# Inverse square roots as one power instruction on GpSimd, and sums of squares and low parts on VectorE, in a hybrid decoder step

## The chip, the cores and the metric

The kernel runs on one core of a Trainium2 chip. The metric is the device time of one execution in microseconds. Three runs of the kernel before took 2132.26, 2138.02 and 2140.12 us; their median, 2138.02 us, is the time before. All figures in the profile are microseconds unless marked ns.

The engines are named as in the profile: PE is TensorE (PEld its weight loads), DVE is VectorE, ACT is ScalarE, POOL is GpSimd, SP is SyncE, which only issues DMAs here.

## The reference

One inference step of one decoder layer, for 512 prompt rows and 32 sample rows (8 sequences of 4) of width 1024. With `pre` and `post` as RMS norms:

```python
def rmsnorm(x, g):
    y = x * lax.rsqrt(jnp.mean(x * x, axis=-1, keepdims=True) + EPS)
    return y * g

h = h + 0.5 * rmsnorm(swiglu(rmsnorm(h, ffn1_pre_g), wg, wu, wd), ffn1_post_g)
u = rmsnorm(h, mix_pre_g)
z, xbc, dt, q, k, v, qi, ki, wi, g_ssd, g_att = split(u @ w_in)
y_ssd = ssd_branch(...)      # state-space scan; ends in an RMS norm over each of 8 groups of 256
y_att = attn_fn(...)         # indexer picks keys, then sparse attention
merged = sigmoid(g_ssd) * (y_ssd @ w_br_ssd) + sigmoid(g_att) * (y_att @ w_br_att)
h = h + rmsnorm(merged @ w_out, mix_post_g)
h = h + rmsnorm(mem_attend(rmsnorm(h, mem_pre_g), ...) @ w_mo, mem_post_g)
h = h + 0.5 * rmsnorm(swiglu(rmsnorm(h, ffn2_pre_g), wg, wu, wd), ffn2_post_g)
```

The outputs are the 544 rows of `h`, and the new keys, values, indexer keys, states and memory keys and values. Every `lax.rsqrt` above is a place that this change touches.

## The kernel before, in words

The 544 rows (512 prompt, 32 sample) lie along the free axis, the 1024 channels as 8 tiles of 128 partitions: `hT` and `y` are 128x8x544. Two column ranges, `HALF = ((0, 256), (256, 288))`, are worked on one after the other wherever one stage's tail overlaps the next stage's head.

Matmuls run in float32r with a split into high and low parts: for each weight tile and each activation tile three matmuls (high x high, high x low, low x high) go into one PSUM bank (`mm`, L320). A weight block comes by DMA (L277), ScalarE rounds it to the high part (L280) and VectorE subtracts to get the low part (L281). Activations are split by `split` (L328 on ScalarE, L329 on VectorE or, where an engine is passed in, on GpSimd).

The norms go by sums of squares over the partition axis. ScalarE squares a tile, and `sq_acc` (L373 to L380) adds the squares of the 8 channel tiles into one accumulator: the first tile is squared straight into it (L376), the following six are squared into one of two scratch tiles `sqt` (L379) and added on GpSimd, and the last is added on VectorE (L380). The accumulators are `sqf` (of a projection's output, filled from `down_half` and `project`) and `sqh` (of the new residual, filled from `bound`). Then `rms_rows` (L421) has TensorE sum the accumulator over its partitions (`sth`, L429), VectorE scales it and adds EPS (L434, L436), and `rsqrt` (L332) takes the inverse root of a 128x2 or 128x3 tile. `spread` (L440) puts the root on the diagonal (L448) and has TensorE spread it over the partitions (`pgr`, L449). `bound` (L382) scales `y` with it (L395), adds it to `hT` (L396) and does the same again for the norm that follows. After that second norm it either writes the factor to `rt` (L409), with the unscaled high and low parts made on the way (L401, L402), or, in the first feed-forward's tail alone, scales `hT` by it (L413) and splits the result (L414); of those 8 low parts the ones of k = 3 and 7 are made on GpSimd.

`rsqrt` works on VectorE alone: a guess from the bits (L336), minus half of x (L337), and three Newton rounds of three instructions (L339 to L341), each of which needs the one before. It is called 25 times: by `row_factor` for both halves of the first norm (L525), once for the memory rows (`row_norm`, L570), by `rms_rows` 14 times, and by `rms` (L343) once in each of the 8 groups of the state-space branch, where the tile is 128x5 and the result goes into a 128x512 diagonal (L362) and a 32x32 one (L364). The last call is in the second feed-forward's tail (`end` in `last_rows`), where the root feeds the six output instructions (L2046) directly.

GpSimd does, besides the additions: indirect DMA gathers of indexer keys (L733) and of selected keys and values (L1645), small copies around the convolution (L1341, L1346, L1347), and fills with zero.

The order of the work is set twice. In the program, generators are woven together: each `yield c, d` says that `c` us of TensorE time were put out and that the generator wants to be taken up again after `d` us (`weave`, L104). `spread` asks for 4.2 us between the root and its spreading, `rms` for 4 or 7. After that the framework plans the order of the instructions on each engine from their dependences, so that instructions of other generators can stand between the steps of one root, or one can be put off. On the engine itself the order is fixed: an instruction that waits holds up those behind it.

Of the kernel before, what the change touches and what calls it, by code (L numbers as in the profile page):

```python
# [7 lines left out]
F32 = mybir.dt.float32  # L8
F32R = mybir.dt.float32r
BF16 = mybir.dt.bfloat16  # L10
I32 = mybir.dt.int32
U32 = mybir.dt.uint32
AF = mybir.ActivationFunctionType
ALU = mybir.AluOpType
# [3 lines left out]
P = 128  # L18
# [150 lines left out]
class Net:  # L169
# [13 lines left out]
    def setup(self):  # L183
        nc, I = self.nc, self.I
        self.cp = cp = self.pool("cp")
        self.wp = self.pool("wp")
        self.pg = self.pool("pg", bufs=2, space=PSUM)
        self.pm = self.pool("pm", bufs=4, space=PSUM)
        self.dr = self.pool("dr", space=DRAM)
        self.ident = cp.tile([P, P], F32, name="ident")  # L190
        self.tri = cp.tile([P, P], F32, name="tri")
        self.caus = cp.tile([P, P], F32, name="caus")
        self.ones = cp.tile([P, P], F32, name="ones")
        nc.sync.dma_start(self.ident, I["ident"])
        nc.vector.memset(self.ones, 1.0)
        self.uh = cp.tile([P, 8, T], F32R, name="uh")
        self.ul = cp.tile([P, 8, T], F32R, name="ul")
        self.xs = [(self.uh[:, k, :], self.ul[:, k, :]) for k in range(8)]
        self.open_y()
        self.open_h()  # L200
# [130 lines left out]

    def rsqrt(self, y, x, xh, t):  # L332

        nc = self.nc
        yi, xi = y.bitcast(I32), x.bitcast(I32)
        nc.vector.tensor_scalar(yi, xi, -0.5, float(0x5F3759DF), op0=ALU.mult, op1=ALU.add)  # L336
        nc.vector.tensor_scalar(xh, x, -0.5, None, op0=ALU.mult)  # L337
        for _ in range(3):
            nc.vector.tensor_tensor(t, y, y, op=ALU.mult)  # L339
            nc.vector.tensor_tensor(t, t, xh, op=ALU.mult)  # L340
            nc.vector.scalar_tensor_tensor(y, t, 1.5, y, op0=ALU.add, op1=ALU.mult)  # L341

    def rms(self, sqs, inv_n, pool, late=4.0):  # L343

# [28 lines left out]
    def sq_acc(self, acc, x, n, first, last=False):  # L373
        nc = self.nc
        if first:
            nc.scalar.activation(acc[:, :n], x, AF.Square)  # L376
        else:
            s = self.sq_tile()
            nc.scalar.activation(s[:, :n], x, AF.Square)  # L379
            (nc.vector if last else nc.gpsimd).tensor_tensor(acc[:, :n], acc[:, :n], s[:, :n], op=ALU.add)  # L380

    def bound(self, half, sq, post_g, pre_g, rt=None):  # L382


        nc, hT, y = self.nc, self.hT, self.y
        r0, n = HALF[half]
        sl = slice(r0, r0 + n)
        if post_g is not None:
            yield 0.0, 3.0
            r = yield from self.rms_h(sq, half)  # L390
        if pre_g is not None:
            acc = self.nw.tile([P, 288], F32, tag="sqh", name="sqh", bufs=2)
        for k in range(8):
            if post_g is not None:
                nc.vector.scalar_tensor_tensor(y[:, k, sl], y[:, k, sl], post_g[:, k:k + 1], r, op0=ALU.mult, op1=ALU.mult)  # L395
                nc.vector.tensor_tensor(hT[:, k, sl], hT[:, k, sl], y[:, k, sl], op=ALU.add)  # L396
            if pre_g is not None:
                self.sq_acc(acc, hT[:, k, sl], n, k == 0, last=(k == 7))
            if rt is not None:
                g = pre_g[:, k:k + 1]  # L400
                nc.scalar.activation(self.uh[:, k, sl], hT[:, k, sl], AF.Copy, scale=g)  # L401
                nc.vector.scalar_tensor_tensor(self.ul[:, k, sl], hT[:, k, sl], g, self.uh[:, k, sl].bitcast(F32), op0=ALU.mult, op1=ALU.subtract)  # L402
            yield 0.0, 1.0
        if pre_g is None:
            return
        yield 0.0, 4.0 if rt is None else 8.0
        r = yield from self.rms_h(acc, half)
        if rt is not None:
            nc.scalar.copy(rt[:, sl], r)  # L409
            return  # L410
        for k in range(8):
            u = self.nw.tile([P, 288], F32, tag="u", name="u", bufs=2)
            nc.vector.scalar_tensor_tensor(u[:, :n], hT[:, k, sl], pre_g[:, k:k + 1], r, op0=ALU.mult, op1=ALU.mult)  # L413
            self.split(self.uh[:, k, sl], self.ul[:, k, sl], u[:, :n], nc.gpsimd if k % 4 == 3 else None)  # L414
            yield 0.0, 0.9

    def rms_h(self, acc, half):
# [1696 lines left out]
```

## Time and profile before

| | us |
|---|---|
| median of three runs | 2138.02 |
| the profiled execution's own time | 2156.45 |
| span of its instructions | 2154.5 |
| POOL busy in it | 300.3 |
| ACT busy in it | 973.4 |
| mean granted TensorE clock (share of full speed) | 0.988 |

The profiled execution is a single one and took 18.4 us more than the median of the runs; outside its span lie 2.0 us. In the page's parts, a group of instructions is named by line, engine, operation and tile, as in `L380 POOL TENSOR_TENSOR sqf<-sqf,sqt`; behind the bar stand its busy time, the mean of one in ns, and the idle time of the engine just before it with what ended most of it. In the rows of a tile or a line, three numbers with slashes are the least, the median and the greatest duration in ns. The chain of waits is followed back from the last instruction: each piece has a start, a length, and the engine, tile and line. A timeline row has start and length, and a wait before it in square brackets.

The stages by time: first feed-forward to about 484, projections, selection of keys and prompt attention to about 880, the state-space groups and the sample rows' attention to about 1372, merging to about 1493, output projection and memory attention to about 1710, second feed-forward to the end.

### The profile page before, as it was taken

To read this page: it belongs to the slowest core of one execution; us is meant where nothing else is said; L and a number is where in the kernel's file an instruction comes from. 1 tells how busy PE (TensorE), PEld (TensorE's weight loads), DVE (VectorE), ACT (ScalarE), POOL (GpSimd) and SP (SyncE) were. 2 spreads that over 40 slices of the span, in tenths; PEclk is the share of its full clock that TensorE was granted. 3 is DMA by queue.
4 is the path that set the end of the run, shared out by engine and by line. 5 is a ranking of instruction groups with operands and counts; after the bars stand their busy time and mean duration, and the time that the engine had idled before them with its cause. 6 is when DMAs were issued, how large, how long until landed. Compare 5 with 4: busy or idle time off the path is not lost.

```text
span 2154.5 us, 41265 instructions
## 1 busy us (share of the span) xinstructions
PE 2088.2 (97%) x16725; PEld 1953.6 (91%) x16725; DVE 1308.9 (61%) x2751; ACT 973.4 (45%) x1856; POOL 300.3 (14%) x373
## 2 busy tenths in 40 slices
PE   9999999999999999999899999999999989999998
PEld 8999999999878779997888889899987889999998
DVE  7533333476788879996677678543663485424455
ACT  6323345344546775453545455322545343222233
POOL 0000011032000001005454620000210210000011
PEclk9999999998999999999999999999999999999999
DMA  6324556357442324446456546554444433233243
GB/s 214 118 84 130 169 197 209 105 137 213 152 131 85 90 78 118 139 133 192 131 169 178 163 146 195 177 171 145 170 147 153 141 118 118 87 101 95 67 134 102
DMA packets 320106, 301.70 MB, mean 140 GB/s; under 512 B 25416, under 2 KB 290632, under 8 KB 318868
## 3 DMA queue, kind: packets, MB, share of 16 engines
q1 hardware_dynamic: 308204, 268.12, 40.5%
q0 software_dynamic: 8448, 25.18, 3.8%
q10 hardware_dynamic: 3264, 5.77, 0.7%
q8 instruction: 132, 2.16, 0.4%
q14 instruction: 58, 0.48, 0.1%
HBM read 261.14 MB, written 37.35 MB: 139 GB/s over the span
## 4 chain that ended last, share of the span: by engine, by line
PE 81%; DVE 8%; DMA 4%; ACT 4%; issue 2%; another core or an unknown queue 1%; POOL 0%; SPq 0%; DVEq 0%; ACTq 0%; POOLq 0%
PE pg L320 45%; PE pgh L320 19%; PE pmo L607 2%; DVE wl L281 2%; DMA abc<-ac_d 1%; PE pqk L1219 1%; PE ph L1465 1%; DVE XO L1353 1%; DMA yt<-yssd_d 1%; PE ppv L1253 1%; PE pmo L1906 1%; PE pmkT L1839 1%; ACT wh L280 1%; PE pkT L1671 1%
## 5 line engine op out<-in xcount | busy, mean ns | idle before, releaser
L280 ACT CAST wh<-wr 128x1024 fp32r<-128x1024 f32 (+3 forms) x362 | 342.0, 959 | 517.1 <-PE pg L320 251.7
L281 DVE TENSOR_TENSOR wl<-wr,wh 128x1024 fp32r<-128x1024 f32 (+3 forms) x362 | 405.6, 1132 | 215.9 <-ACT wh L280 209.8
L320 PE MATMUL pg<-uh,wh 128*128 128x256 f32 (+1 forms) x2336 | 499.4, 295 | 1.8 <-ACT CB L1344 1.7
L320 PE MATMUL pg<-uh,wl 128*128 128x256 f32 (+1 forms) x2336 | 490.3, 290 | 0.7 <-issue 0.7
L320 PE MATMUL pg<-ul,wh 128*128 128x256 f32 (+1 forms) x2336 | 488.5, 290 | 0.0
L320 PEld LDWEIGHTS pg<-uh,wh 128*128 128x128 f32 x2336 | 377.1, 189 | 21.2 <-issue 16.5
L320 PEld LDWEIGHTS pg<-ul,wh 128*128 128x128 f32 x2336 | 377.7, 189 | 3.3 <-issue 2.8
L320 PEld LDWEIGHTS pg<-uh,wl 128*128 128x128 f32 x2336 | 376.9, 189 | 2.4 <-issue 2.0
L320 PE MATMUL pgh<-uh,wl 128*128 128x256 f32 (+2 forms) x880 | 257.5, 295 | 3.9 <-DVE wl L281 3.8
L320 PE MATMUL pgh<-uh,wh 128*128 128x288 f32 (+2 forms) x880 | 259.0, 297 | 2.1 <-ACT uh L328 2.1
L320 PE MATMUL pgh<-ul,wh 128*128 128x256 f32 (+1 forms) x880 | 255.7, 292 | 0.0
L320 PEld LDWEIGHTS pgh<-uh,wl 128*128 128x128 f32 (+1 forms) x880 | 168.1, 192 | 6.5 <-DVE wl L281 5.0
L320 PEld LDWEIGHTS pgh<-uh,wh 128*128 128x128 f32 (+1 forms) x880 | 168.4, 192 | 4.9 <-ACT uh L328 2.7
L320 PEld LDWEIGHTS pgh<-ul,wh 128*128 128x128 f32 x880 | 169.5, 193 | 1.4 <-issue 0.8
L380 POOL TENSOR_TENSOR sqf<-sqf,sqt 128x256 f32<-128x256 f32 (+1 forms) x48 | 54.6, 1137 | 521.2 <-ACT sqt L379 509.3
L320 PE MATMUL pgh<-hh,wh 128*128 128x288 f32 (+1 forms) x352 | 101.6, 289 | 0.0
L320 PE MATMUL pgh<-hl,wh 128*128 128x288 f32 (+1 forms) x352 | 100.9, 287 | 0.0
L320 PE MATMUL pgh<-hh,wl 128*128 128x288 f32 (+1 forms) x352 | 100.9, 287 | 0.0
L1353 DVE SCALAR_TENSOR_TENSOR XO<-CB,convw,XO 128x600 f32<-128x600 f32 x96 | 80.3, 837 | 14.1 <-ACT XO L1351 13.5
L633 DVE TENSOR_TENSOR g<-pg,rt 128x544 f32<-128x544 f32 x32 | 23.2, 725 | 102.7 <-PE pg L320 102.7
L639 DVE TENSOR_TENSOR g<-pg,g 128x544 f32<-128x544 f32 x32 | 23.2, 725 | 97.1 <-PE pg L320 97.1
L1645 POOL DMA_INDIRECT kv<-in_cache_v,slot x64 | 70.4, 1101 | 34.6 <-issue 13.1
(606 smaller groups left out, 3679.1 us busy)
## 6 DMA issues: line engine op xcount, KB each, us to landing
wr<-in_w_in SPq DMA_DIRECT2D x66, 512.0 KB
wr<-in_ffn_wg SPq DMA_DIRECT2D x48, 512.0 KB
wr<-in_ffn_wu SPq DMA_DIRECT2D x48, 512.0 KB
wr<-in_ffn_wd SPq DMA_DIRECT2D x44, 384.0 KB
wr<-in_ffn_wd SPq DMA_DIRECT2D x44, 320.0 KB
kt_d<-KT SPq DMA_DIRECT2D x8, 1024.0 KB
KT<-kt_d SPq DMA_DIRECT2D x16, 512.0 KB
wr<-in_w_in SPq DMA_DIRECT2D x32, 256.0 KB
```

Source lines behind the costliest of these rows:

```text
L280: nc.scalar.copy(hi[:, s], r)
L281: (lo_eng or nc.vector).tensor_tensor(lo[:, s], r, hi[:, s].bitcast(F32), op=ALU.subtract)
L320: nc.tensor.matmul(o, a[:, k, c0:c0 + m], x[:, r0:r0 + n], start=(k == 0 and j == 0), stop=(k == KT - 1 and j == 2))
L380: (nc.vector if last else nc.gpsimd).tensor_tensor(acc[:, :n], acc[:, :n], s[:, :n], op=ALU.add)
L607: nc.tensor.matmul(ps[:, :256], a[:, k, i * P:(i + 1) * P], b[:, k, :], start=(k == 0 and j == 0), stop=(k == 7 and j == 2))
L633: nc.vector.tensor_tensor(g1[:, :n], pg, rt[:, sl], op=ALU.mult)
L639: nc.vector.tensor_tensor(g1[:, :n], pu, g1[:, :n], op=ALU.mult)
L1219: nc.tensor.matmul(ps[:, :W], qT[hb:hb + 64, h // 2, i * P:(i + 1) * P], ks[hb:hb + 64, gp, :W], start=True, stop=True)
L1253: nc.tensor.matmul(ps[g2 * 64:(g2 + 1) * 64, :], V[:, j, g * 64:(g + 1) * 64], PTs[j][:, g2, :], start=(j == 0), stop=(j == i))
L1353: nc.vector.scalar_tensor_tensor(xo, CB[:, j:j + 600], cw(j), xo, op0=ALU.mult, op1=ALU.add)
L1465: nc.tensor.transpose(ps[:, b * P:(b + 1) * P], h0[n // 2][:, n % 2 * 4 + b, :], self.ident)
L1645: nc.gpsimd.indirect_dma_start(out=t[:, hf, :], out_offset=None, in_=(pk, pv)[x], in_offset=off)
```

## The change

`rsqrt` becomes one instruction on GpSimd: x to the power of a constant tile that holds -0.5, filled once at the start. `sq_acc` adds all its squares on VectorE. The low parts of k = 3 and 7 in `bound` are made on VectorE, as the others were. The callers still reserve the tiles `xh` and `t`, which nothing uses any more. The waits that the generators ask for are unchanged.

```diff
@@ setup
         nc.vector.memset(self.ones, 1.0)
+        self.power = cp.tile([P, 8], F32, name="power")
+        nc.vector.memset(self.power, -0.5)
@@ rsqrt
     def rsqrt(self, y, x, xh, t):
 
-        nc = self.nc
-        yi, xi = y.bitcast(I32), x.bitcast(I32)
-        nc.vector.tensor_scalar(yi, xi, -0.5, float(0x5F3759DF), op0=ALU.mult, op1=ALU.add)
-        nc.vector.tensor_scalar(xh, x, -0.5, None, op0=ALU.mult)
-        for _ in range(3):
-            nc.vector.tensor_tensor(t, y, y, op=ALU.mult)
-            nc.vector.tensor_tensor(t, t, xh, op=ALU.mult)
-            nc.vector.scalar_tensor_tensor(y, t, 1.5, y, op0=ALU.add, op1=ALU.mult)
+        self.nc.gpsimd.tensor_tensor(y, x, self.power[:, :x.shape[1]], op=ALU.pow)
@@ sq_acc
             s = self.sq_tile()
             nc.scalar.activation(s[:, :n], x, AF.Square)
-            (nc.vector if last else nc.gpsimd).tensor_tensor(acc[:, :n], acc[:, :n], s[:, :n], op=ALU.add)
+            nc.vector.tensor_tensor(acc[:, :n], acc[:, :n], s[:, :n], op=ALU.add)
@@ bound
             nc.vector.scalar_tensor_tensor(u[:, :n], hT[:, k, sl], pre_g[:, k:k + 1], r, op0=ALU.mult, op1=ALU.mult)
-            self.split(self.uh[:, k, sl], self.ul[:, k, sl], u[:, :n], nc.gpsimd if k % 4 == 3 else None)
+            self.split(self.uh[:, k, sl], self.ul[:, k, sl], u[:, :n])
```

## Prediction

> **What bounds the kernel now.** I read the page first, then the busy time by stretches, then the chain of work that ended last, and last the timelines of VectorE and GpSimd around each inverse root.
>
> ```profile
> span 2154.5 us, 41265 instructions
> ...
> PE 2088.2 (97%) x16725; PEld 1953.6 (91%) x16725; DVE 1308.9 (61%) x2751; ACT 973.4 (45%) x1856; POOL 300.3 (14%) x373
> ...
> PE 81%; DVE 8%; DMA 4%; ACT 4%; issue 2%; another core or an unknown queue 1%; POOL 0%; SPq 0%; DVEq 0%; ACTq 0%; POOLq 0%
> ```
>
> TensorE is busy for 2088.2 of 2154.5 us. The change leaves every matmul alone, so its gain can come only out of the 66.3 us in which TensorE stands still, and out of the matmuls that run late without showing as idle. The chain says the same: 81% TensorE, 8% VectorE. GpSimd is on it for less than 0.5%.
>
> ```profile
> 484.00:530.00 46.00, 42.67 (x281) 40.55 (x281) 32.78 (x83) 23.06 (x46) 11.93 (x16) 0.82 0.64 196
> 978.00:1268.00 290.00, 273.31 (x2387) 238.60 (x2386) 197.93 (x464) 143.44 (x299) 153.55 (x184) 0.99 0.57 170
> 1709.00:1733.00 24.00, 21.92 (x168) 21.31 (x166) 23.44 (x46) 15.93 (x34) 12.63 (x12) 1.00 0.49 139
> ```
>
> The columns after the length are the busy times of TensorE, its weight loads, VectorE, ScalarE and GpSimd. In the norm stretch from 1709 to 1733 VectorE is busy for 98% of the time, and from 484 to 530, where another norm lies, TensorE stands still for 3.3 us: these are the places where VectorE's work decides. From 978 to 1268 it is busy for 198 of 290 us, and GpSimd, with the gathers, for 154.
>
> **The Newton steps go.** Each inverse root is 11 small VectorE instructions, one behind the other.
>
> ```profile
> L336 DVE TENSOR_SCALAR nw<-nw x24: 146/170/682, 19.7 to 2145.5; 128x2 int32<-128x2 int32 x8, 128x3 int32<-128x3 int32 x8, 128x5 int32<-128x5 int32 x8
> ```
> ```profile
> 2145.53 0.17 DVE L336 TENSOR_SCALAR nw<-nw 128x3 int32<-128x3 int32 x1
> ...
> 2147.31 0.16 DVE L341 SCALAR_TENSOR_TENSOR nw<-nw 128x3 f32<-128x3 f32 x1
> 2147.59 0.75 DVE L2046 SCALAR_TENSOR_TENSOR fo<-yr,nw,hr 128x512 f32<-128x512 f32 x1
> ```
>
> With that of `row_norm`, on another tile, there are 24 + 1 = 25 roots. Undisturbed, one takes from 2145.53 to 2147.47, 1.94 us; the 25 free some 48 us of VectorE. Only where the root is on the chain does that shorten the run. In the chain of waits I find L336 at five places (with the root's reader where the steps are drawn out):
>
> ```profile
> 508.37 0.17 DVE nw L336
> ```
> ```profile
> 1034.29 0.08 DVE nw L336
> ```
> ```profile
> 1110.44 0.17 DVE nw L336
> ```
> ```profile
> 1117.15 0.61 DVE zt L362
> ```
> ```profile
> 1728.22 0.59 DVE nw L336
> ```
> ```profile
> 1733.01 0.30 DVE dg L448
> ```
> ```profile
> 2145.53 0.17 DVE nw L336
> ```
>
> The other 20 lie beside matmuls that the generators and the planner put there; I cost their removal at nothing. If that cover were gone, each would be worth what the five are.
>
> **What a power costs.** The trace of before has no power. The nearest rows on GpSimd:
>
> ```profile
> L1346 POOL COPY ncv<-CB 128x3 f32<-128x3 f32 x32 | 13.2, 413 | 124.0 <-ACT CB L1343 123.4 <-issue 0.5
> ```
> ```profile
> L380 POOL TENSOR_TENSOR sqf<-sqf,sqt x48: 721/1132/2317, 420.9 to 2137.1; 128x256 f32<-128x256 f32 x24, 128x288 f32<-128x288 f32 x24
> L380 POOL TENSOR_TENSOR sqh<-sqh,sqt x36: 735/888/1716, 457.1 to 1763.1; 128x256 f32<-128x256 f32 x18, 128x288 f32<-128x288 f32 x18
> ```
>
> A copy of three columns takes 0.41 us in the mean, an addition of 256 or 288 columns 0.72 at least, 1.13 in the median and 2.32 at most. A power of two to five columns does little data and much arithmetic a column; I take 0.7 us, between the copy and the median addition, and keep 0.4 and 2.3 as the ends that rows give. The handing over shows here:
>
> ```profile
> 501.19 0.45 ACT sqt L379
> ...
> 501.77 0.82 POOL sqh L380
> ...
> 505.85 0.89 POOL sqh L380
> ...
> 506.76 0.47 DVE sqh L380
> ```
>
> ScalarE ends at 501.64 and GpSimd starts at 501.77 (0.13); GpSimd ends at 506.74 and VectorE starts at 506.76 (0.02). So a root would take 0.13 + 0.7 + 0.02 = 0.85 us in place of 1.94, a gain of 1.1 where nothing else is late. At 508 and at 2145 the reader of the root follows at once, and nothing else waits: -1.1 each. At 1728 the root is stretched to 4.79 us by two weight casts and an addition that stand between its steps; that work remains, and is late next, so I take -1.0. At 1034 and 1110 casts, convolution steps and GpSimd's gathers lie around it: -0.3 each. Sum: -3.8 us. With 0.4 us for the power the five give -3.8 - 5 x 0.3 = -5.3 us, with 2.3 they give -3.8 + 5 x 1.6 = +4.2.
>
> GpSimd sets itself up anew ahead of its first arithmetic on two tensors:
>
> ```profile
> L380 POOLq MODIFY_POOL_CONFIG x2: 37/37/37, 363.2 to 363.3; - x2
> ```
>
> The first addition followed at 420.9, as the row of L380 says, so 57 us covered whatever that takes. The first power stands at the first root, at 19.7 us (row of L336), with nothing on GpSimd ahead of it but fills, so I cost it at nothing; if the cover is too short, the start gets longer by what is missing.
>
> **The additions and low parts come over.** 48 + 36 = 84 additions (L380) and 4 low parts (L329) move.
>
> ```profile
> L380 DVE TENSOR_TENSOR sqf<-sqf,sqt x8: 426/436/458, 443.9 to 2141.7; 128x256 f32<-128x256 f32 x4, 128x288 f32<-128x288 f32 x4
> ```
>
> At VectorE's 0.44 us, 88 of them are 39 us, against 48 freed. They also give time back, since they now slow VectorE down:
>
> ```profile
> 504.65 1.42 DVE L396 TENSOR_TENSOR hT<-hT,y 128x288 f32<-128x288 f32 x2
> ```
> ```profile
> 1748.39 0.82 DVE L396 TENSOR_TENSOR hT<-hT,y 128x288 f32<-128x288 f32 x2
> ...
> 1753.00 1.99 DVE L396 TENSOR_TENSOR hT<-hT,y 128x288 f32<-128x288 f32 x2
> ```
> ```profile
> 1752.89 3.72 POOL L380 TENSOR_TENSOR sqh<-sqh,sqt 128x288 f32<-128x288 f32 x4 [1.72 <-ACT sqt L379]
> ```
>
> The same pair of VectorE additions takes 0.82 us alone and 1.99 or 1.42 beside GpSimd's. One addition on VectorE (0.44) thus costs about what one on GpSimd takes from VectorE where they meet ((1.99 - 0.82) / 2 = 0.6, (1.42 - 0.82) / 2 = 0.3), so a stretch of 98% gets no fuller. What is gained is the tail. VectorE ends its last pair at 504.65 + 1.42 = 506.07; the square of it on ScalarE (0.45) and the handing over put the last addition at some 506.6, where GpSimd's backlog, each addition in front of the next, lets it start at 506.76. I take -0.2 us, and as much for each of the six tails of this kind (two norms in each of the three `bound`s that go on to another norm), -1.2 us. The ends are -4, if each were worth the 0.6 of one meeting addition, and +3, if each addition cost VectorE its 0.44 and nothing came back in the last one of each tail. The four low parts are additions of the same size; I take nothing for them.
>
> The Trainium skill, page "SBUF — State Buffer", section "Who interferes with whom", says that a VectorE instruction with two SBUF inputs and a GpSimd instruction that reads SBUF shut each other out for their whole length. The trace agrees, with 1.99 beside 0.82. The rule also speaks against this change, since a power reads SBUF as well. By it the casts at 1110 and 1728 would stand still for the 0.7 us of a power, and the sum would be 1.4 us worse.
>
> **The wait that is added.** The reader of each root (L448, L362, L572 or L2046) now waits on VectorE for GpSimd, and behind it VectorE's whole queue waits, the weight casts L281 that feed TensorE too. GpSimd in turn holds its gathers behind a power whose input is late.
>
> **Sum.** -3.8 - 1.2 = -5.0 us on the profiled execution's 2156.45: 2151.4. That execution was 0.9% above the median of the runs (2138.02), so I scale: 2151.45 x 2138.02 / 2156.45 = 2133.1 us, -0.23%. A measurement of this kernel can tell about 0.5% (10.7 us) from no change.
>
> **Rivals.**
>
> *VectorE's relief reaches the chain in full (2124 us, 0.20).* If casts and steps that stand between Newton steps close up, the root at 1728 falls from 4.79 to 0.85 (-3.9), that at 1110 from 1110.44 to 1117.15 by some -5, that at 1034 by -1; with -2.2 for 508 and 2145 and -2 for the tails that is -14 us. For it: VectorE's 98% in 1709 to 1733. Against it: that work doesn't vanish, and TensorE is at 97%.
>
> *A slow power (2158 us, 0.18).* It decides from 1.94 - 0.15 = 1.8 us on. GpSimd may work through a power step by step, a column at a time. At 6 us, above the 4.2 that the generator of `spread` plans for the root, the five places lose 6.15 - 1.94 = 4.2 each: +21, less 1.2, +20 us on 2156.45. At such a length some of the 20 hidden ones come out too. For it: no row bounds a power from above. Against it: only two to five columns.
>
> *The power waits in GpSimd's queue (2153 us, 0.10).*
>
> ```profile
> L1645 POOL DMA_INDIRECT kv<-in_cache_v,slot x64 | 70.4, 1101 | 34.6 <-issue 13.1 <-PE pkT L1671 11.5 <-PE pO L1715 6.9
> ```
> ```profile
> 1069.12 0.94 POOL L1645 DMA_INDIRECT kv<-in_cache_k,slot  x1 [12.62 <-PE pkT L1671]
> ```
>
> A gather takes 1.1 us, and one stood for 12.62 us until TensorE had freed a buffer. Of the five roots on the chain those of 1034 and 1110 lie among gathers. If each stood behind eight of them or such a wait, some 10 us, VectorE's queue would stand with it: +20, less 4.4 of the other terms, +15.6 on 2156.45. Against it: the planner puts the power where its input comes.
>
> *It does nothing that can be seen (2138 us, 0.07):* the instructions are planned anew, and the gains are spent on another order.
>
> **How the numbers follow.** My forecast has 0.45. Faster by over 0.5% comes from most of the first rival and a little of the forecast: 0.22. Slower by over 0.5% comes from most of the second and third: 0.23. Within it: 0.55. The range of 2120 to 2158 takes in the first rival with 4 us beyond, and the slow power up to 6 us; what is left out is a power much longer than that, and a relief beyond 18 us.
>
> **What would show it.** Right: one GpSimd instruction of 0.4 to 1.2 us at each of the 25 places; VectorE near 1309 - 48 + 39 = 1300 us busy, less what the stretched pairs give back; L396 pairs all near 0.8; at the end less than 1.2 us between L436 and L2046. Wrong: a power above 1.8 us; VectorE waiting for GpSimd at L362 with gathers ahead of the power; or TensorE's idle time below 52 us.

## The result, and the profile after

| | median, us | lowest to highest | runs |
|---|---|---|---|
| before, beside it | 2138.23 | 2132.26 to 2140.12 | 6 |
| after | 2119.27 | 2117.20 to 2122.93 | 6 |

The ratio is 0.9922, with a 95% interval of 0.9907 to 0.9938: 0.8% faster. The forecast was 2133.1 us with a range of 2120 to 2158; the result is 0.7 us below its lower end. The sign was right and the size was not: some 17 to 19 us in place of 5.

The page of the changed kernel, its span, its busy times and the shares of its chain:

```profile
span 2117.2 us, 40949 instructions
...
PE 2075.4 (98%) x16725; PEld 1946.1 (92%) x16725; DVE 1278.3 (60%) x2565; ACT 972.3 (46%) x1856; POOL 234.5 (11%) x310
...
PE 83%; DVE 6%; DMA 5%; ACT 3%; issue 2%; POOL 0%; SPq 0%; DVEq 0%; POOLq 0%; ACTq 0%
```

The execution of before that the prediction read took 2156.45 us, more than any of the runs. So I took a second profile of before (the run e0_before_again below, 2134.31 us), and all comparisons from here on are with that one:

```profile
span 2131.7 us, 41265 instructions
...
PE 2081.8 (98%) x16725; PEld 1951.2 (92%) x16725; DVE 1309.4 (61%) x2751; ACT 972.5 (46%) x1856; POOL 301.5 (14%) x373
...
PE 84%; DVE 7%; DMA 4%; ACT 2%; issue 2%; POOL 0%; SPq 0%; DVEq 0%; ACTq 0%; POOLq 0%
```

TensorE stands still for 2131.7 - 2081.8 = 49.9 us there (the prediction read 66.3) and for 41.8 us after. That is 8.1 of the 14.5 us between the two spans. The other 6.4 us are busy time: the same 16725 matmuls took that much less. The reader who looks only at idle time misses them.

The stretches that the prediction chose, first of the second profile of before, then of the changed kernel. Behind the length stand the busy times of TensorE, weight loads, VectorE, ScalarE and GpSimd, then the granted clock of TensorE:

```profile
484.00:530.00 46.00, 41.72 (x290) 40.02 (x289) 33.70 (x84) 23.03 (x46) 12.86 (x16) 0.86 0.65 196
978.00:1268.00 290.00, 289.17 (x2594) 256.18 (x2594) 217.45 (x503) 154.41 (x324) 160.00 (x194) 1.00 0.60 178
1709.00:1733.00 24.00, 23.01 (x185) 22.07 (x184) 18.92 (x52) 12.85 (x22) 2.75 (x4) 1.00 0.48 140
```
```profile
484.00:530.00 46.00, 42.53 (x308) 40.89 (x308) 31.61 (x74) 24.38 (x49) 4.99 (x8) 0.93 0.66 206
978.00:1268.00 290.00, 287.23 (x2580) 254.11 (x2579) 210.97 (x459) 154.03 (x326) 161.78 (x196) 1.00 0.59 175
1709.00:1733.00 24.00, 22.01 (x178) 21.23 (x177) 22.83 (x48) 13.98 (x27) 0.00 (x0) 1.00 0.48 143
```

From 978 to 1268 TensorE was idle for 16.7 us in the execution that the prediction read, and is idle for 0.8 and 2.8 us here. Two of the five roots that I priced lay there, in a stretch that is long in that execution and not in these two; e0 says where it is long again. Between 484 and 530 the clock column moves from 0.86 to 0.93, and TensorE gets through 308 matmuls in place of 290.

Where the time goes can be read from when the same instructions start. Each time is the start of a TensorE instruction in its own profile, us:

| | first `pqk` (attention) | last `pfin` (state-space stage) | first `pms` (memory attention) | span |
|---|---|---|---|---|
| before, second profile | 662.7 | 1327.0 | 1585.7 | 2131.7 |
| roots alone (e1) | 660.1 | 1325.1 | 1586.0 | 2130.3 |
| additions and low parts alone (e2) | 661.9 | 1326.8 | 1579.5 | 2125.0 |
| after | 657.8 | 1322.7 | 1575.2 | 2117.2 |
| after, second profile (e14) | 654.3 | 1318.1 | 1570.3 | 2111.9 |

The changed kernel gains 4.9 and 8.4 us up to the attention, about nothing in the state-space stage, some 6 to 7 us between 1327 and 1586, and 4 us behind it. The gains lie in the stretches that hold the norms over the rows; the stage that holds eight of the 25 roots gains nothing.

**The clock.** Each trace also records when TensorE's clock is granted at half. It happens in windows of 3.41 us (or a whole number of these), mostly at or just behind a place where TensorE stands still for 1.2 to 3.9 us; the one at 556 us lies among small matmuls without such a gap. Not every gap is followed by a window: those of 1.94 us at 1522 and 1.81 us at 1703 in the second profile of before are not. Ahead of 2100 us the second profile of before has 13 such windows, the two profiles of the changed kernel 8 and 6. The largest group lies at 510 us: three or four windows in the profiles of before and of the kernels with one part of the change (e1, e2, e3, e13), one and none in those of the changed kernel. The variants of the changed kernel have none (e7), one (e10, e11) or three (e5, e9). Columns of each row: length, busy TensorE, granted clock, share of the transfer engines, GB/s. First before, then after, then after's second profile:

```profile
510.00:515.00 5.00, 3.65 (x14) 0.52 0.78 266
515.00:520.00 5.00, 4.66 (x19) 0.50 0.66 162
```
```profile
510.00:515.00 5.00, 3.71 (x21) 0.81 0.65 250
515.00:520.00 5.00, 5.00 (x38) 1.00 0.95 332
```
```profile
510.00:515.00 5.00, 3.71 (x27) 1.00 0.78 250
515.00:520.00 5.00, 5.00 (x38) 1.00 0.97 378
```

And the matmuls that start between 515.5 and 520 us, of before and of after (minimum, median and maximum in ns):

```profile
L320 PE MATMUL pgh<-uh,wh x8: 442/442/606, 515.3 to 519.1; 128*128 128x288 f32 x8
```
```profile
L322 PE MATMUL pgh<-ul,wh x12: 293/294/393, 515.3 to 519.8; 128*128 128x288 f32 x12
```

The same kind of matmul takes 442 ns in one and 294 in the other, and 19 against 38 of them go through in 5 us. All of it is booked as busy time.

Each run lists its span and its mean granted clock, so the loss can be counted without a profile, as (1 - mean clock) x span. That is an upper bound, since half a clock costs nothing while TensorE waits, and the clock is listed to 0.001 only, which is 2 us a run. It is worked out for the experiments below, always against the runs of before beside them.

**The power.** GpSimd's new instruction, by its number of columns (count, total us, mean ns; then GpSimd's idle time ahead of it):

```profile
L336 POOL TENSOR_TENSOR nw<-nw,power 128x5 f32<-128x5 f32 x8 | 9.6, 1196 | 65.2 <-DVE nw L351 65.0
L336 POOL TENSOR_TENSOR nw<-nw,power 128x3 f32<-128x3 f32 x8 | 6.9, 860 | 137.0 <-DVE nw L431 134.2 <-DVE nw L519 2.8
L336 POOL TENSOR_TENSOR nw<-nw,power 128x2 f32<-128x2 f32 x8 | 6.5, 816 | 576.9 <-DVE nw L428 386.8 <-DVE nw L429 170.7 <-DVE nw L519 19.3
```

The least of each form is 0.70, 0.85 and 1.16 us, and the longest of all took 1.61, with two columns, beside a weight cast of VectorE:

```profile
1697.17 1.61 POOL L336 TENSOR_TENSOR nw<-nw,power 128x2 f32<-128x2 f32 x1 [22.14 <-DVE nw L429]
```
```profile
1697.01 1.22 DVE L283 TENSOR_TENSOR wl<-wr,wh 128x1024 fp32r<-128x1024 f32 x1
```

The last root of the run, on VectorE and GpSimd:

```profile
2109.41 0.14 DVE L431 TENSOR_SCALAR nw<-sth 32x1 f32<-32x1 f32 x1
2109.69 0.85 POOL L336 TENSOR_TENSOR nw<-nw,power 128x3 f32<-128x3 f32 x1 [39.17 <-DVE nw L431]
2110.58 0.75 DVE L2041 SCALAR_TENSOR_TENSOR fo<-yr,nw,hr 128x512 f32<-128x512 f32 x1 [1.03 <-POOL nw L336]
```

From the input's end (2109.55) to the reader it takes 0.14 + 0.85 + 0.04 = 1.03 us. Counted the same way it took 2.09 us before (2145.50 to 2147.59); the 1.94 of the prediction leaves out the handing over at both ends.

### The profile page after: what moved, and what is told of

The parts are those of the page before. It is cut to its first block, busy times and chain, and to the rows that moved or that the text cites. A ratio compares the mean times of both kernels' runs of the same rounds, so it can differ in the third digit from the quotient of the medians.

```text
span 2117.2 us, 40949 instructions
## 1 busy us (share of the span) xinstructions
PE 2075.4 (98%) x16725; PEld 1946.1 (92%) x16725; DVE 1278.3 (60%) x2565; ACT 972.3 (46%) x1856; POOL 234.5 (11%) x310
## 4 chain that ended last, share of the span: by engine, by line
PE 83%; DVE 6%; DMA 5%; ACT 3%; issue 2%; POOL 0%; SPq 0%; DVEq 0%; POOLq 0%; ACTq 0%
PE pg L322 46%; PE pgh L322 20%; PE pmo L602 2%; DVE wl L283 1%; PE pqk L1214 1%; DMA abc<-ac_d 1%; ACT wh L282 1%; DMA wr<-in_w_in 1%; PE pmkT L1834 1%; DVE XO L1348 1%; PE ppv L1248 1%; DMA yt<-yssd_d 1%; PE pmo L1901 1%; DVE eqm L1146 1%; PE ph L1460 1%
## 5 line engine op out<-in xcount | busy, mean ns | idle before, releaser
L283 DVE TENSOR_TENSOR wl<-wr,wh 128x1024 fp32r<-128x1024 f32 (+3 forms) x362 | 397.3, 1110 | 215.7 <-ACT wh L282 213.1
L322 PE MATMUL pgh<-uh,wh 128*128 128x256 f32 (+2 forms) x880 | 256.1, 294 | 3.6 <-ACT uh L330 2.5
L336 POOL TENSOR_TENSOR nw<-nw,power 128x2 f32<-128x2 f32 (+2 forms) x24 | 23.0, 957 | 779.1 <-DVE nw L428 386.8
```

Of the source, the lines that this page charges most:

```text
L283: (lo_eng or nc.vector).tensor_tensor(lo[:, s], r, hi[:, s].bitcast(F32), op=ALU.subtract)
L322: nc.tensor.matmul(o, a[:, k, c0:c0 + m], x[:, r0:r0 + n], start=(k == 0 and j == 0), stop=(k == KT - 1 and j == 2))
L336: self.nc.gpsimd.tensor_tensor(y, x, self.power[:, :x.shape[1]], op=ALU.pow)
```

## The experiments

The theories are named in the expectations. N: the gain comes from the roots. A: it comes from GpSimd losing the additions. P: any edit makes another plan, and the gain is luck. C: shorter or filled waits save half-clock windows of TensorE. K: only the idle time itself counts.

| kernel | ratio to before | 95% interval | clock loss against before beside it, us | rest of the span, us |
|---|---|---|---|---|
| e0 before again | 1.0005 | 0.9991 to 1.0018 | +1.4 | -0.1 |
| e1 roots alone | 0.9966 | 0.9953 to 0.9978 | -7.1 | +0.7 |
| e2 additions and low parts alone | 0.9972 | 0.9960 to 0.9983 | -3.9 | -2.3 |
| e3 roots of the state-space stage alone | 1.0006 | 0.9992 to 1.0021 | -0.1 | +0.9 |
| e13 a third of the additions | 0.9987 | 0.9978 to 0.9997 | -1.3 | -1.3 |
| e7 after, low parts on GpSimd | 0.9918 | 0.9904 to 0.9933 | -9.5 | -8.0 |
| e14 after again | 0.9920 | 0.9905 to 0.9936 | -9.5 | -8.5 |
| e10 after, one root by Newton steps | 0.9941 | 0.9923 to 0.9960 | -7.8 | -5.5 |
| e5 after, every root's power twice | 0.9981 | 0.9971 to 0.9991 | -7.1 | +2.5 |
| e8 before, useless matmuls at 508 | 0.9979 | 0.9967 to 0.9991 | -7.6 | +3.3 |
| e9 after, useless matmuls at four places | 0.9913 | 0.9897 to 0.9929 | -12.8 | -5.7 |
| e11 after, more of them | 0.9925 | 0.9912 to 0.9939 | -12.5 | -2.3 |

The loss is a mean over 5 to 12 runs of a kernel, and over 9 to 35 of before, where it is 25 to 29 us; from run to run it scatters by 2 to 4 us. The two kernels e7 and e11 ran on a chip on which every kernel took some 15 to 20 us more (before 2153.19 us), so only their ratios say something.

**e0: before, without an edit.**

> This is the kernel before, without an edit, for a second profile of it. Every theory: the same time as before, 2132 to 2141 us, a ratio of 0.998 to 1.002. It is there for the comparison of stages: the profiled execution of before took 2156.45 us and its chain holds 10.87 us behind 'another core or an unknown queue' at 1047.52, which the changed kernel's chain does not have. If that row belongs to one execution and not to the kernel, the second profile lacks it and its span is some 2134 to 2140 us; if it belongs to the kernel, the row comes back and the span is again near 2150.

2136.31 us against 2134.21 beside it. The second profile has no wait for another core in its chain, and its span is 2131.7. So the row and the 16.7 us of idle time from 978 to 1268 do not belong to every execution. They came back on one chip: e7 and e11 ran where before took 2149.66 to 2155.70 us, and there TensorE is idle in this stretch for 13.1 us (e7) and 14.4 us (e11). The row in the first profile of before, and the row and the stretch in e11:

```profile
1047.52 10.87 another core or an unknown queue
```
```profile
1051.41 10.34 another core or an unknown queue
```
```profile
978.00:1268.00 290.00, 275.58 (x2425) 241.23 (x2424) 197.77 (x430) 143.89 (x300) 160.19 (x192) 0.99 0.59 173
```

The first profile of before, with its 2156.45 us, looks like an execution on such a chip; on which it ran is not on record, nor what the wait is for.

**e1: the roots alone.**

```
-        (the eleven VectorE instructions)
+        self.nc.gpsimd.tensor_tensor(y, x, self.power[:, :x.shape[1]], op=ALU.pow)
```

> The kernel before with the inverse roots by the power instruction alone; the additions of squares and the last low parts stay on GpSimd. Theory N (the gain of 19 us comes from the roots: eleven small instructions, which VectorE runs among its casts, become one of 0.7 to 1.2 us): most of the gain is here, 2121 to 2128 us, ratio 0.992 to 0.995. Theory A (the gain comes from the additions of squares leaving GpSimd, whose instructions stretch VectorE's beside them): only the 4 us that the forecast gave the roots, 2132 to 2136 us, ratio 0.997 to 0.999. Theory P (any edit makes another plan of the weaving of steps, and the gain is the luck of the plan): no sum of parts; this could come out at either value, or above 1.

2127.78 us; by the ratio 7 us, between what N and A expected. By the count over the runs the whole of it is clock; the rest of the span moves by +0.7 us, within the scatter. The profile agrees on the idle time: 2130.3 - 2080.8 = 49.5 us, as in before. That profile is of an execution with 13 windows and so shows little of the gain; its clock of 0.988 is at the low end of the twelve runs, whose mean is 0.991.

**e2: the additions and low parts alone.**

```
-            (nc.vector if last else nc.gpsimd).tensor_tensor(acc[:, :n], acc[:, :n], s[:, :n], op=ALU.add)
+            nc.vector.tensor_tensor(acc[:, :n], acc[:, :n], s[:, :n], op=ALU.add)
...
-            self.split(self.uh[:, k, sl], self.ul[:, k, sl], u[:, :n], nc.gpsimd if k % 4 == 3 else None)
+            self.split(self.uh[:, k, sl], self.ul[:, k, sl], u[:, :n])
```

> The kernel before with the additions of squares and the last low parts on VectorE; the roots stay eleven VectorE instructions. Theory N: little, between 2133 and 2138 us, ratio 0.998 to 1.000 (about the 1 us of the six tails, and 39 us more of VectorE work beside the Newton steps). Theory A: most of the gain, 2120 to 2127 us, ratio 0.992 to 0.995; the casts beside no GpSimd addition at 0.8 us and not 1.4 to 2.0. Theory P: no sum with the run of the roots alone.

2128.84 us; by the ratio 6 us. Neither N nor A alone holds; the two halves save about the same. Together 13 us, against 17 for the changed kernel. With these intervals that may be a plain sum (0.9966 x 0.9972 = 0.9938), or hold a few us that only both bring. The profile shows TensorE's waits go. Waits of TensorE in before (us in total, times, longest), then of ScalarE:

```profile
PE sth L429 <- DVE sqh L380: 5.0, 3, 1.8
...
PE pmkT L1839 <- ACT mkT__16923 L1840: 1.9, 1, 1.9
```
```profile
ACT sqt L379 <- POOL sqf L380: 4.5, 5, 1.8
```

and TensorE's with the additions moved:

```profile
PE sth L429 <- DVE sqh L380: 2.0, 1, 2.0
```

Before, TensorE waits three times for the last sum of squares. ScalarE waits five times to square, since the two buffers of squares (`sqt`) are still held by GpSimd's additions, and what it does next waits with it. At 1522 us TensorE's transposes (`pmkT`) wait 1.9 us for a late copy of ScalarE's. With the additions on VectorE one wait of 2.0 us for a sum is left, at 505 us; the other two, that of `pmkT` and those of ScalarE are gone.

**e3: the power in the eight norms of the state-space stage alone** (the tiles of five columns).

```
+        if x.shape[1] == 5:
+            self.nc.gpsimd.tensor_tensor(y, x, self.power[:, :x.shape[1]], op=ALU.pow)
+            return
```

> The kernel before with the power instruction in the eight normalisations of the state-space stage alone (the tiles of five columns); the other 17 roots stay on VectorE, the additions on GpSimd. Theory N: the traces put some 16 of the 19 us in the stretch from 880 to 1370 us, where these eight roots lie, so 2124 to 2130 us, ratio 0.993 to 0.996, and the rest of the roots bring what is left. Theory A: 0 to 2 us, ratio 0.999 to 1.000, as these normalisations have no GpSimd additions of their own. Theory P: no relation to the stretch.

2136.55 us: nothing that shows. N expected the gain here because the first profile of before was slow in this stage; N falls in that form. The other 17 roots bring the 7 us. That this edit changes the program and moves nothing speaks against P.

**e13: the last three additions of each sum on VectorE.**

```
-                self.sq_acc(acc, hT[:, k, sl], n, k == 0, last=(k == 7))
+                self.sq_acc(acc, hT[:, k, sl], n, k == 0, last=(k >= 5))
```

(and the same in the two other callers.)

> The kernel before with the last three additions of each sum of squares on VectorE instead of the last one alone (28 of GpSimd's 84 additions move; the low parts and the roots stay). The run with all additions on VectorE took 0.9972 of before. In the second profile of before TensorE waited 5.0 us in three places for a sum (sth behind sqh), and ScalarE 4.5 us for squares' buffers that GpSimd still held; with all additions moved 2.0 us and nothing. If GpSimd's backlog at the end of a sum is what cost, moving its last links brings all of that: the wait at sth falls to about 2 us, ratio 0.996 to 0.998. If it is each addition's own slowness (0.8 to 1.5 us each, holding buffers and stretching VectorE), a third of it: ratio 0.9985 to 0.9995, and the waits at sth stay at 4 to 5 us.

2132.35 us: 0.13% with 28 of the 84, where all of them and the low parts brought 0.28%. The waits fall from 5.0 and 4.5 us to 2.8 each. TensorE's and ScalarE's:

```profile
PE sth L429 <- DVE sqh L380: 2.8, 2, 1.4
```
```profile
ACT sqt L379 <- POOL sqf L380: 2.8, 3, 1.8
```

So it is not the last link alone, and a third of the additions brought somewhat under half of the gain. The interval (0.03% to 0.22%) takes in a third as well, and does not settle the share.

**e7: the changed kernel with every fourth low part back on GpSimd.** The edit is the line of `split` in e2, undone.

> The changed kernel with the last low parts of normalised rows (every fourth subtraction) back on GpSimd; the additions of squares stay on VectorE, the roots on the power instruction. The forecast gave these low parts 0: 2119 us, ratio 0.992. If the 6 us that the run with additions and low parts alone saved came in part from the low parts, 2120 to 2123 us, ratio 0.9925 to 0.994; if the sum tails at 1557 and 1703 us (1.7 and 1.8 us of idle time ahead of sth<-ones,sqh in the second profile of before) are those of the additions, they stay away here.

The ratio is 0.9918 against 0.9920 and 0.9922 of the changed kernel: the low parts are worth nothing that shows.

**e14: the changed kernel again.**

> The changed kernel without an edit, for a second profile and more runs beside one another. Every theory: the ratio to before again 0.9907 to 0.9938. Theory C: the clock's mean over the runs again above before's by 0.004 to 0.005 (0.992 against 0.987 to 0.988), which is 9 us of half-clock windows, and the rest of the span 6 to 7 us shorter; the second profile has seven to ten half-clock windows. If the nine windows fewer were the luck of one profile, the mean clock comes out within 0.001 of before's while the time stays.

2118.43 us, 0.9920. The clock's mean is 0.9927 against 0.9883, 15.5 against 25.0 us lost, and the rest of the span is 8.5 us shorter. So about half of the gain is clock, and the other half is what is left for shorter waits; the fewer windows are not one profile's luck.

**e10: Newton steps at one root of the changed kernel**, the fourth that `rms_rows` makes, at 508 us.

```
+        self.nth += 1
-        self.rsqrt(y, x, xh, t)
+        self.rsqrt(y, x, xh, t, self.nth == 3)
```

> The changed kernel with the eleven Newton instructions back at one root alone, the one at 508 us ahead of the second layer's attention. The forecast gave this root 1.1 us of the chain: 2120.4 us, ratio 0.9925 to 0.993. Theory C: the 1.7 us of idle time behind the sums come back, and with them two half-clock windows at 510 us, 1.7 us of work each, so 4 to 5 us: 2123 to 2125 us, ratio 0.9935 to 0.995, with three windows there and the clock's mean down by 0.001 to 0.002.

2123.34 us; 0.9941 against 0.9922 and 0.9920, so some 4 us for this root where I had 1.1. The intervals of the two kernels still overlap. What TensorE waits for between 503 and 518 us, in before, in the changed kernel and in this one:

```profile
PE pgr L449 <- DVE dg L448: 1.7, 1, 1.7
PE sth L429 <- DVE sqh L380: 1.5, 1, 1.5
```
```profile
PE sth L424 <- DVE sqh L375: 1.7, 1, 1.7
PE pgh L322 <- ACT uh L330: 1.3, 1, 1.3
```
```profile
PE pgr L456 <- DVE dg L455: 1.7, 1, 1.7
PE sth L435 <- DVE sqh L386: 1.6, 1, 1.6
```

With the steps TensorE waits 1.6 us for the sums and then another 1.7 for the spreading of the root (`pgr`). With the power the second wait is covered by the transposes that stand there (in its second profile 0.7 us of it is left). Two gaps close to each other become one. But this profile has one window here and not three or four. e1's has three with waits of only 1.1 and 0.6 us, and e9's three with the second wait alone. So the number of windows does not follow the length of these waits from one execution to the next, and how the 4 us come about at this root is not shown.

**e5: two powers one behind the other at every root.**

```
+        self.nc.gpsimd.tensor_tensor(t, x, self.one[:, :x.shape[1]], op=ALU.pow)
-        self.nc.gpsimd.tensor_tensor(y, x, self.power[:, :x.shape[1]], op=ALU.pow)
+        self.nc.gpsimd.tensor_tensor(y, t, self.power[:, :x.shape[1]], op=ALU.pow)
```

> The changed kernel with a second power instruction (to the power 1, so the result stays) chained ahead of each of the 25, which adds 0.7 to 1.2 us to every root. By the forecast's own steps, five roots lie on the chain: 5 x 0.7 to 0.9 = 3.5 to 4.5 us, so 2123 to 2124 us, ratio 0.9935 to 0.995, the clock's mean unchanged at 0.992. Theory C: the same idle time and three to six more half-clock windows, 2127 to 2134 us, ratio 0.995 to 0.9985, the clock's mean at 0.988 to 0.990. If VectorE's relief were all that counts (the root's own length hidden), nothing: 2119 to 2120 us.

2132.15 us, 13 us more than the changed kernel: inside C's range, three times what the forecast's count of roots gives. But little of it is clock (2 to 5 us, by the series compared), and 8 to 11 us are the rest of the span: C's mechanism is not what costs here. The roots of the state-space stage have come out: from the first `pqk` to the last `pfin` it takes 1334.6 - 661.0 = 673.6 us, against 1322.7 - 657.8 = 664.9; two half-clock windows in that stretch (at 965 and 1101 us), which the changed kernel's profiles lack, are up to 3.4 us of the difference. TensorE's waits for a root's readers, in the changed kernel and here:

```profile
PE psr L360 <- DVE zt L357: 0.9, 1, 0.9
PE pgr L444 <- DVE dg L443: 0.8, 3, 0.4
```
```profile
PE pgr L447 <- DVE dg L446: 6.0, 6, 1.6
PE psr L363 <- DVE zt L360: 2.5, 2, 2.1
```

**e8: before, with useless matmuls on TensorE at 508 us.** Nobody reads them; the outputs come from the same work as in before. (`fill` issues `matmul(out, ones, ident)` into unused columns of a tile.)

```
+        self.fill(st[:, 384:512], {3: 2}.get(self.nth["rows"], 0))      # ahead of the sums
+        self.fill(st[:, 256:384], {3: 2}.get(self.nth["rows"], 0))      # behind them
+        self.fill(ps[:, 384:512], {5: 1}.get(self.nth["spread"], 0))    # behind the spreading
```

> The kernel before, with five matmuls that nobody reads put on TensorE at one place, around the root at 508 us: two ahead of the sums of the squares, two behind them, one behind the spreading of the root (each of the form that took 0.6 us as pgr<-dg,ones). The arithmetic of the outputs is that of before, eleven Newton instructions and all. Theory C (clock): the trace grants TensorE half its clock for windows of 3.41 us behind its idle stretches; three windows stand at 510 us in the second profile of before, one in the changed kernel. If that is what a shorter root saves, work put into the idle time saves it too: the windows at 510 fall from three to one or none, and the time by 2 to 5 us, ratio 0.9975 to 0.999. Theory K (chain: only the idle time itself counts): nothing is saved, and the useless work delays by 0 to 1 us, ratio 1.000 to 1.0005.

2132.91 us, 0.9979: useless work saves 4 us. (The 0.6 us of the expectation were those of two such matmuls, so the five are 1.5 us and not 3.) The windows at 510 are gone in the profile, and the matmuls run as after. The rows of 510 to 520 us, and the matmuls from 515.5 us:

```profile
510.00:515.00 5.00, 2.37 (x16) 1.00 0.80 268
515.00:520.00 5.00, 4.88 (x32) 1.00 0.78 250
```
```profile
L321 PE MATMUL pgh<-uh,wh x12: 293/296/400, 515.3 to 519.9; 128*128 128x288 f32 x12
```

Over the runs the clock's loss falls by 7.6 us and the rest of the span grows by 3.3. TensorE's waits here are no shorter in all: 1.0 + 1.8 + 1.3 = 4.1 us, against 1.5 + 1.7 + 0.9 = 4.1 in the second profile of before. By this profile it is work put between the waits that saved the clock, and not less idle time. K expected no saving at all; C holds.

**e9 and e11: the changed kernel with useless matmuls at more places** (behind the spreadings at 480 and 513 us, and ahead of and in the first groups of the state-space output projection, where TensorE waits 3.88 and 2.33 us; e9 also at 506 us).

```
+        self.fill(ps[:, 384:512], {3: 2, 5: 2}.get(self.nth["spread"], 0))     # e11: 4 and 4
-            ps = result(self.mm(w, ys, 0))
+            ps = result(self.mm(w, ys, 0, fill={0: (0, 6), 1: (2, 3)}.get(m, (0, 0))))   # e11: 11 and 7
```

> The changed kernel with 15 such matmuls that nobody reads: two at 506 us ahead of the sums, two at 480 and two at 513 us behind a root's spreading, six ahead of the first matmul of the state-space output projection (idle 3.88 us at 1358.7) and three in its second group (idle 2.33 us at 1379.4). Theory C: of the changed kernel's eight half-clock windows five (one at 484.6, one at 508.5, two at 1361.8, one at 1382.3) lie at these places; three to five go, 1.7 us each, so 2111 to 2115 us, ratio to before 0.989 to 0.991. Theory K: nothing to gain, 2119 to 2121 us, ratio 0.992 to 0.993.

> The changed kernel with more of the useless matmuls, which cost 0.3 us each (four records of pgr took 0.6 us for two of them), and none ahead of the sums at 506 us, where the run before put two and the transposes behind them came ahead of the sums: four behind the spreading at 480 us and four at 513 us, eleven ahead of the first matmul of the state-space output projection (idle 3.88 us), seven inside its second group (2.33 us). Theory C: the windows at 484.6, 1361.8 (two) and 1382.3 go, 1.7 us each and no idle time is added: 2112 to 2116 us, ratio 0.989 to 0.991, the clock's mean at 0.994 to 0.995. If the clock counts for less (the stretches behind these places wait for transfers anyway), the clock's mean rises and the time stays at 2117 to 2120 us.

0.9913 and 0.9925, against 0.9922 and 0.9920: neither is told apart from the changed kernel, and neither reaches the 0.989 to 0.991 that C expected. The clock's loss is 14.5 us in e9, where the changed kernel has 15.5 and 16.9 in its two series, but the rest of the span gives that back. In e9 the order around 508 us changed (the transposes came ahead of the sums), and the root's 1.7 us of waiting were back; in e11 the gap at 480 us grew from 1.24 to 2.62 us, since the next matmuls' operand (`uh`, from ScalarE) came later: they start 3.5 us behind the spreading and not 1.2. So filling paid at one place of before, and here it cost about what it saved. No version here is shown to beat the changed kernel.

## Why the prediction was wrong in size, point by point

- **The power's price: right.** 0.7 us was taken for every root; it is 0.70 us undisturbed with two columns, 0.85 with three, 1.20 with five. The last root takes 1.03 us where it took 2.09 counted the same way, so it saves the 1.1 of the sum.
- **The roots, -3.8 us: mis-sized; e1 measured 7.** The failing step is that a root on the chain was given the time by which it gets shorter ("a gain of 1.1 where nothing else is late") and nothing for the clock. By the count over the runs all of e1's gain is clock. At 508 us the root got about 1 us shorter, and TensorE's second wait went from 1.7 us to nothing and to 0.7 in the two profiles of the changed kernel, with one and no half-clock window behind it in place of three. Since e1's own profile has three there, the link at this place is argued and not shown. The terms of 1034 and 1110 brought nothing that shows in e3; its interval leaves room for -0.3 each, but not for the -6 of the first rival at the same places.
- **"Matmuls that run late without showing as idle": named, and given no term.** The row of 484 to 530 us that the prediction quoted carried a granted clock of 0.82 in it, up to 18% of 46 us, and no step used it. About half of the gain is this term.
- **The six tails, -0.2 each: mis-sized.** I read one tail, at 506 us, where GpSimd's backlog was short; that one stays (1.5 before, 1.7 after). Two other tails cost TensorE 1.7 and 1.8 us, and ScalarE's 4.5 us of waiting for the buffers of squares stood in the waits of before. All of that goes. With the clock behind it, e2 is 6 us where I had 1.2.
- **The additions return what they cost VectorE: right for nearly all of it.** 88 more instructions raised VectorE's busy time by 1314.7 - 1309.4 = 5.3 us in e2, and not by 39. The additions of L396 on 288 columns take 599 ns in the mean in the second profile of before and 451 after:

```profile
L396 DVE TENSOR_TENSOR hT<-hT,y 128x288 f32<-128x288 f32 x24 | 13.6, 599 | 0.0
```
```profile
L391 DVE TENSOR_TENSOR hT<-hT,y 128x288 f32<-128x288 f32 x24 | 10.2, 451 | 0.0
```

  In the whole VectorE is busy for 1278 us, where the prediction had 1300 less what is given back.
- **Low parts at nothing: right** (e7). **GpSimd's set-up at nothing: right;** it stands at 0.7 us, 19 us ahead of the first power.
- **The wait that is added.** VectorE does wait at almost every root, mostly for about 1 us:

```profile
DVE dg L443 <- POOL nw L336: 11.4, 14, 1.0
DVE zt L357 <- POOL nw L336: 6.9, 6, 1.3
```

  That is 18.3 us, and the run got shorter. The longest is 1.3 us, so no gather held a power up by much, and the third rival falls. Beside 17 of the 25 powers VectorE ran nothing, and beside one alone it ran a weight cast, the one at 1697 us: the cast took the 1.22 us of its form's mean, and the power 1.61 in place of 0.70. The prediction worked out 1.4 us of held-up casts by the rule of the Trainium skill ("SBUF — State Buffer", "Who interferes with whom"). The trace shows none of that: where the two met, it was the power that took longer.
- **The rivals.** The first came nearest with 2124 us, for a reason that the runs don't show. The slow power fell, but its bound was about right: e5, with roots of some 1.9 us with three columns and 2.6 with five, keeps 0.9981, no more than the additions alone bring (e2, 0.9972).
- **What would prove it wrong** was an idle time of TensorE below 52 us. It came out at 41.8; but before itself has 49.9 in its second profile, so the bound, drawn from the one slower execution, could not tell the two kernels apart.

That TensorE's clock falls behind its gaps is also told by the Trainium skill, "TensorE: Matmul & The Clock Gate", section "HAM oscillation — how this bites in real kernels": no idle gaps above about 3.4 us. The traces agree on halves of the clock and on 3.41 us for a window. They differ on the gap: windows stand behind single gaps of 1.2 us (at 480.6) and 2.1 us (at 617.2) in before's second profile. What makes the one at 556 us, where no gap stands, why three windows follow at 510 in some executions and one or none in others, and by which places the roots alone save clock, stays open.

## What to carry to other kernels

An engine's idle gap has a second price where the clock of TensorE falls behind it: read the granted clock beside the busy time in each stretch, and give the matmuls that run at half of it a term of their own. Work between two short waits can be worth more than its length: five useless matmuls of 1.5 us saved 4 us here with the waits as long as before. Small helper instructions on a slow engine cost less by their own time than by what they hold: a buffer that ScalarE wants next, and VectorE's instructions beside them. Before a stretch is priced from one profile, look whether a second execution, on another chip too, has it.

## What the runs showed that was not expected

- Useless matmuls made a kernel faster: 0.9979 (0.9967 to 0.9991) with five of them.
- The mean granted clock differs from run to run of the same kernel (0.985 to 0.991 in 35 runs of before), and with it the time by several us.
- GpSimd's power on two, three and five columns of 128 partitions takes 0.70, 0.85 and 1.20 us: by these three some 0.36 us and another 0.17 a column.
- The kernel's time depends on the chip: before took 2134 to 2138 us on some and 2153 on another. The profiles on that one (e7, e11) take 679.6 and 682.4 us from the first `pqk` to the last `pfin`, the stage with the gathers, where the changed kernel's two take 664.9 and 663.8; the first profile of before took 687.9.
